# Projected keys and queries through DRAM scratch: heads outermost against one row per head and feature

## The chip, the cores and the metric

One Trainium2 chip, one of its cores. The metric is the device time of one execution in microseconds (us), as the median of several runs; lower is better. The engines are TensorE (PE, its weight loads PEld), VectorE (DVE), ScalarE (ACT), GpSimd (POOL) and SyncE (SP), which here only issues DMAs. Sixteen DMA engines move the data.

## The reference

One layer of a decoder over 512 tokens of width 1024, in float32: a SwiGLU half-step, then a mixer, then a second SwiGLU half-step, a gated per-layer embedding and a last norm. The change lies in the mixer, whose projections are:

```python
z = rmsnorm(h, norm_mix[i]) @ w_in[i]
q, kc, vc, ksl, vsl, kw, vw, g, u = jnp.split(z, split_at, axis=-1)
q = rope(q.reshape(B, L, N_HEADS, HEAD_DIM), pos)       # 8 heads x 64
kc, ksl, kw = rope(...)                                  # 2 heads x 64 each
o_nsa = nsa_attention(q, kc, vc, ksl, vsl, kw, vw, gates, pe_k, pe_v, wk1, wk2, wv1, wv2)
o_s5 = s5_mixer(u, ...)
h = h + concatenate([o_nsa, o_s5]) @ w_out[i]
```

`rope` turns features r and r + 32 of a head (a pair) against each other. Attention has three branches with the same queries: over compressed blocks of keys (`kc`, through a small two-layer network `compress`), over selected blocks (`ksl`) and over a window (`kw`). Scores are dot products over the 64 features of a head, so any order of the features gives the same scores as long as queries and keys share it. `compress` multiplies keys by rows of `wk1`, so its rows, the position table and the columns of `wk2` have to follow the order too.

## The kernel before, in words

Activations lie with features on partitions and the 512 tokens along the row. Every float32 product is three TensorE passes over operands split into a high and a low part: ACT casts the high part of a weight tile (`hi`, L147), DVE subtracts to get the low part (`lo`, L149), and PE runs `hi*xh`, `hi*xl`, `lo*xh` (`mm3`). Weight tiles come in from `wpack` in the order of use, through a ring of four buffers, issued from ACT's queue.

The mixer (L688 on) begins with the projections. `proj` makes one 128 x 512 product of 24 matmuls. `rotary` (L845) makes two of them, `oa` with the first halves of four heads (partition 32 h + r) and `ob` with the second halves, and forms `a1 = oa cos - ob sin` in buffer `r1` and `a2 = oa sin + ob cos` in `r2` on DVE (L854 to L859). The next products need both halves of one head on the 64 partitions of a contraction, and twice, on partitions 0 to 63 and 64 to 127. That move goes through DRAM: SP stores `a1` and `a2` into a scratch tensor (L860, L861), `kd` for keys and `qd` for queries, and later loads 64 rows at a time back, each twice: `kf` for keys (L868, L869; from these ACT casts `KA`, L870, and DVE makes `KB`, L871) and `qf` for the queries of one block of 128 tokens (L1031, L1032 in `scores`; from these `QA` and `QB`, L1033 to L1035). `cmp_kv` (L875) does the same for the compressed keys (`kcd`, L885) and stores the compressed values to `vcd` (L891); `windows` (L918) loads both back (`cst`, L922, L923).

Before the change the scratch is laid out by feature, then head, then token: `kd[64, 4, 512]`, `qd[64, 8, 512]`, `kcd[64, 2, 512]`. A store of 128 partitions therefore has two strides on the DRAM side, heads outermost:

```python
nc.sync.dma_start(dst[0:32].rearrange("r h t -> h r t"), a1)    # L860, 4 x 32 x 512
nc.sync.dma_start(kcd[32 * half:32 * half + 32].rearrange("r g t -> g r t"), ...)   # L885, 2 x 32 x 512
```

The order of work: keys (`kq`, one `rotary` and four `kf` tiles), queries of heads 0 to 3, the four products of the S5 input (`s5_input`, which stores `ut` to `ud`, L760, and reads it back as `u8` in 16 small loads, L764), queries of heads 4 to 7, then the S5 recurrence woven with `scores(3)`, `scores(2)`, `cmp_kv` and `v_gates`. A scheduler orders the instructions of each engine when the program is built; each engine then runs its list in order, and an instruction that waits holds all behind it on its engine. Buffers `r1` and `r2` are single and are used by every `rotary`, by `qf` of `scores(3)` and by `cst`; `ra` and `ut` have two buffers each.

Of the kernel before, what the change touches and what calls it, by code (L numbers as in the profile page):

```python
# [76 lines left out]
def block_kernel(ctx: ExitStack, tc: tile.TileContext, a: dict, out: bass.AP):  # L77
# [602 lines left out]
    nm = state["n"]  # L680

    ud = dram.tile([512, 8, 64], F32, tag="ud", name="ud")
    qd = dram.tile([64, 8, SEQ], F32, tag="qd", name="qd")
    kd = dram.tile([64, 4, SEQ], F32, tag="kd", name="kd")
    kcd = dram.tile([64, 2, SEQ], F32, tag="kcd", name="kcd")
    vcd = dram.tile([2, 64, SEQ], F32, tag="vcd", name="vcd")

    def mixer(ctx):  # L688
# [156 lines left out]
        def rotary(dst, tag):  # L845
            oa = proj(tag)
            if not hasattr(nm, "rb"):
                nm.finish()
                for t, raw in zip((cosr, sinr), ropes):
                    V.tensor_tensor(t, raw, nm.rb, OP.mult)  # L850
            yield
            ob = proj(tag)
            a1, b1, a2, b2 = (tp.tile([128, SEQ], F32, tag=n, name=n) for n in ("r1", "rb1", "r2", "r3"))
            V.tensor_tensor(a1, oa, cosr, OP.mult)  # L854
            V.tensor_tensor(a2, oa, sinr, OP.mult)
            V.tensor_tensor(b1, ob, sinr, OP.mult)
            V.tensor_tensor(b2, ob, cosr, OP.mult)
            V.tensor_tensor(a1, a1, b1, OP.subtract)
            V.tensor_tensor(a2, a2, b2, OP.add)  # L859
            nc.sync.dma_start(dst[0:32].rearrange("r h t -> h r t"), a1)  # L860
            nc.sync.dma_start(dst[32:64].rearrange("r h t -> h r t"), a2)  # L861
            yield

        def kq():
            yield from rotary(kd, "A")
            for b in range(4):
                kf = mp.tile([128, SEQ], F32, tag="ra", name="kf", bufs=2)
                nc.sync.dma_start(kf[0:64], kd[:, b])  # L868
                nc.sync.dma_start(kf[64:128], kd[:, b])  # L869
                S.copy(KA[:, b], kf)  # L870
                V.tensor_tensor(KB[0:64, b], kf[0:64], KA[0:64, b].bitcast(F32), OP.subtract)  # L871
            yield from rotary(qd[:, 0:4], "B")


        def cmp_kv():  # L875
            o = proj()
            ta = mp.tile([128, SEQ], F32, tag="ra", name="ra", bufs=2)
            tb = tp.tile([128, SEQ], F32, tag="rb1", name="rb1")
            V.tensor_tensor(ta, o, cosr, OP.mult)
            V.tensor_tensor(tb[0:64], o[64:128], sinr[64:128], OP.mult)  # L880
            V.tensor_tensor(tb[64:128], o[0:64], sinr[0:64], OP.mult)
            V.tensor_tensor(ta[0:64], ta[0:64], tb[0:64], OP.subtract)
            V.tensor_tensor(ta[64:128], ta[64:128], tb[64:128], OP.add)
            for half in range(2):
                nc.sync.dma_start(kcd[32 * half:32 * half + 32].rearrange("r g t -> g r t"),  # L885
                                  ta[64 * half:64 * half + 64])
            yield
            o = proj()
            ta = mp.tile([128, SEQ], F32, tag="ra", name="ra", bufs=2)
            V.tensor_tensor(ta, o, nm.rb, OP.mult)  # L890
            nc.sync.dma_start(vcd.rearrange("g d t -> (g d) t"), ta)  # L891
            yield
# [25 lines left out]
        def windows(src, i, dst):  # L918
            ev = []
            for g in range(2):  # L920
                st = tp.tile([128, SEQ], F32, tag=f"r{g + 1}", name="cst")
                nc.sync.dma_start(st[0:64], src[:, g])  # L922
                nc.sync.dma_start(st[64:128, 0:SEQ - 1], src[:, g, 1:SEQ])  # L923
                ev.append(st.rearrange("p (j l r) -> p l j r", l=8, r=2)[:, :, :, 0])
            sp = []
            for half, t in enumerate(dst):
                t = t.rearrange("p (l g j) -> p l g j", l=8, g=2)
                for g in range(2):
                    V.tensor_tensor(t[:, :, g], ev[g],
                                    pe[:, i, 8 * half:8 * half + 8, None].to_broadcast([128, 8, 32]), OP.add)  # L930
                sp.append(t)
            return sp

        def cmp_all():

            kt = [tp.tile([128, SEQ], F32, tag=n, name="cs") for n in ("rb1", "r3")]
            sps = windows(kcd, 0, kt), windows(vcd.rearrange("g d t -> d g t"), 1, (cosr, sinr))
            ps = bank("A", (128, 256))
            for l in range(16):
                if l % 2 == 0:  # L940
                    raw = unit(True)
                lo, n = l // 8, 64 - l // 8
                for i in range(2):
                    xs = sps[i][lo][:, l % 8].rearrange("p g j -> p (g j)")[:, lo:64]
                    w = (2 * i + l % 2) * 256
                    mm(ps[64 * i:64 * i + n], xs, raw[:, w:w + 256], l == 0, l == 15)
                if l % 2:
                    yield
            ht = tp.tile([128, SEQ], F32, tag="r3", name="ht")[:, :256]
            gelu2(ht, ps, 256, "rb1")  # L950
            pt = bank("C", (128, 2, 128))
            for m in range(2):
                PE.transpose(pt[:, m], ht[:, m * 128:m * 128 + 128], ident)
            hid = npool.tile([128, SEQ], F32, tag="acc", name="chid", bufs=1)[:, :256].rearrange("p (m c) -> p m c", m=2)
            S.activation(hid, pt, AF.Copy, scale=0.5)
            hk, hv = hid[:, :, 0:63], hid[:, :, 64:127]
            p = bank("D", (64, 2, 32))
            for m in range(2):
                mm(p.rearrange("p g j -> p (g j)")[:, 0:63], w2[:, 0, m], hk[:, m], m == 0, m == 1)
            p = p[:, :, 0:31]  # L960
            kah = KAc[:, 0:128].rearrange("p (g i j) -> p g i j", g=2, i=2)
            kbl = KBc[:, 0:64].rearrange("p (g j) -> p g j", g=2)
            S.copy(kah[0:64, :, 0, 0:31], p)
            S.copy(kah[64:128, :, 0, 0:31], p)
            V.tensor_tensor(kbl[0:64, :, 0:31], p, kah[0:64, :, 0, 0:31].bitcast(F32), OP.subtract)
            V.tensor_copy(kah[0:64, :, 1, 0:31], kbl[0:64, :, 0:31].bitcast(F32))
            for g in range(2):
                p = bank("D", (31, 64))
                for m in range(2):
                    mm(p, hv[:, m, 32 * g:32 * g + 31], w2[:, 1, m], m == 0, m == 1)  # L970
                S.copy(VLc[0:31, g, 0:64], p)
                V.tensor_tensor(VLc[0:31, g, 64:128], p, VLc[0:31, g, 0:64].bitcast(F32), OP.subtract)
# [47 lines left out]
        def scores(qb, env, pool, tags="B", stage=("ra", "ra")):  # L1020
# [2 lines left out]
            tq = slice(qb * 128, (qb + 1) * 128)  # L1023
            QA = pool.tile([128, 8, 128], FR, tag="QA", name="QA", bufs=2)
            QB = pool.tile([128, 8, 128], FR, tag="QB", name="QB", bufs=2)
            for hs, st in zip((slice(0, 4), slice(4, 8)), stage):
                if st == "ra":
                    qf = mp.tile([128, 4, 128], F32, tag=st, name="qf", bufs=2)
                else:
                    qf = tp.tile([128, 4, 128], F32, tag=st, name="qf")  # L1030
                nc.sync.dma_start(qf[0:64], qd[:, hs, tq])  # L1031
                nc.sync.dma_start(qf[64:128], qd[:, hs, tq])  # L1032
                S.activation(QA[:, hs], qf, AF.Copy, scale=0.125)  # L1033
                V.tensor_scalar(QB[0:64, hs], qf[0:64], 0.125, None, OP.mult)
                V.scalar_tensor_tensor(QA[64:128, hs], qf[64:128], 0.125, QA[64:128, hs].bitcast(F32),  # L1035
                                       OP.mult, OP.subtract)
# [139 lines left out]
        def drain(g):  # L1176
            for _ in g:
                pass
# [5 lines left out]
        s5g, pg, cg, gg = s5_all(), chain(cmp_kv(), v_gates()), cmp_all(), glu()  # L1184
        sg = chain(scores(3, envs[3], mp, TS, G3), scores(2, envs[2], mp, TS, G2))
        drain(s5_input())
        drain(rotary(qd[:, 4:8], "B"))
        table.append(tc.keep_in_program_order(S.preload_act_table_set("exp_and_others")))
        weave((s5g, 17), (sg, S1), (pg, 6))
        drain(s5g)  # L1190
# [161 lines left out]
def _pack_weights(x):  # L1352
# [49 lines left out]
    add(vt[:, 3:6])  # L1402
    add(vt[:, 6:8])
    wk, wv = (x[n][0].reshape(16, 128, 256).transpose(1, 0, 2) for n in ("cmp_wk1", "cmp_wv1"))
    for i in range(8):
        add(np.concatenate([wk[:, 2 * i:2 * i + 2], wv[:, 2 * i:2 * i + 2]], axis=1))
    m_major(x["s5_w_glu"][0], range(4), range(4))
# [4 lines left out]
    m_major(x["w_ple_gate"][0], range(8), range(8))  # L1412
    assert [len(t) // 128 for t in units] == UNIT_W
    return np.concatenate(units)


def _rope_tables():
# [6 lines left out]
def prep(x):  # L1424
# [21 lines left out]
    def pair(r, i):  # L1446
# [2 lines left out]
    sg = np.ones((128, 2), f32)  # L1449
    sg[:64, 0] = -1  # L1450
    sg[64:, 1] = -1
    pe = np.stack([x["cmp_pe_k"][0].reshape(16, 128).T, x["cmp_pe_v"][0].reshape(16, 128).T], axis=1)
    w2 = np.stack([x["cmp_wk2"][0].reshape(2, 128, 64).transpose(1, 0, 2),
                   x["cmp_wv2"][0].reshape(2, 128, 64).transpose(1, 0, 2)], axis=1)
    return {
        "xT": c(x["x"][0].T),
# [37 lines left out]
```

## Time and profile before

| | |
|---|---|
| median of 3 runs | 1091.61 us (1091.03 to 1093.57) |
| the profiled execution | 1090.99 us, of which the span from first to last instruction is 1089.1 us |
| mean granted TensorE clock | 0.985 |
| PE busy | 1042.0 us, 96% |
| DVE busy | 775.2 us, 71% |
| ACT busy | 462.1 us, 42% |
| the stretch of the mixer's projections and scores | about 400 to 545 us |

Busy time of PE counts a matmul at whatever clock it had, so a stretch at half clock is busy too. Of a timeline the start of each instruction says most: where two matmuls of the same kind start 0.227 us apart, the clock is the upper level; where they start 0.43 us apart, it is the lower. The share of the DMA engines is a mean over sixteen, so one engine busy all the time is 0.06.

### The profile page before, as it was taken

The page shows a single profiled execution, that of the slowest core. Times are in us where ns is not written, and L with a number is a line of the kernel's source. Part 1 is how long each engine was busy: PE and PEld are TensorE (multiplying, and loading weights), DVE is VectorE, ACT ScalarE, POOL GpSimd, SP SyncE. Part 2 cuts the span into 40 slices and gives each one's busy share as a digit, 9 for nine tenths or more (in the row PEclk, how much of TensorE's full clock was granted, in tenths as well). Part 3 has the DMA queues.
Part 4 walks back from the last instruction along what each step waited for, and adds up shares of the span by engine and source line. Part 5 has one row for each costly group of instructions (what it writes and reads, how often), then busy time and mean ns, then how long its engine had stood idle before and what let it go on. Part 6 is the DMA issues. An engine that isn't in the chain of part 4 may idle for free.

```text
span 1089.1 us, 15119 instructions
## 1 busy us (share of the span) xinstructions
PE 1042.0 (96%) x5854; PEld 881.4 (81%) x5854; DVE 775.2 (71%) x1328; ACT 462.1 (42%) x786; POOL 163.9 (15%) x187
## 2 busy tenths in 40 slices
PE   7999999999999998899799999999999999999995
PEld 6888888888888886676577668799899899899895
DVE  6995455445447764689788977997598678687766
ACT  6222233123222522236657875555256245245541
POOL 4006056435628200000000000000000000000000
PEclk9999999999999999999799999999999999999998
DMA  7333225336734835758121004333333423424402
GB/s 251 120 102 109 89 93 171 97 97 168 170 95 129 280 104 158 189 174 294 39 69 48 1 20 145 93 113 115 97 101 102 128 78 100 133 79 149 137 6 78
DMA packets 48596, 128.48 MB, mean 118 GB/s; under 512 B 10300, under 2 KB 17052, under 8 KB 47500
## 3 DMA queue, kind: packets, MB, share of 16 engines
q10 hardware_dynamic: 26080, 90.51, 26.5%
q0 software_dynamic: 4336, 17.60, 6.1%
q1 hardware_dynamic: 18108, 19.40, 5.7%
q8 instruction: 46, 0.75, 0.3%
q14 instruction: 26, 0.21, 0.1%
HBM read 111.99 MB, written 15.73 MB: 117 GB/s over the span
## 4 chain that ended last, share of the span: by engine, by line
PE 78%; DVE 8%; DMA 5%; issue 4%; ACT 4%; SPq 0%; POOLq 0%; POOL 0%; ACTq 0%; DVEq 0%
PE ps_C L126 24%; PE ps_A L126 23%; PE ps_B L126 21%; PE ps_D L126 10%; DMA kf<-kd 1%; DVE nmax L1053 1%; DMA kd<-r 1%; DVE lo L149 1%; DMA qd<-r 1%; ACT e L743 1%; DMA qf<-qd 1%; ACT eh L743 1%; ACT ps_B L743 1%; DMA cst<-vcd 1%; DVE el L1148 0%
## 5 line engine op out<-in xcount | busy, mean ns | idle before, releaser
L147 ACT CAST hi<-raw 128x1024 fp32r<-128x1024 f32 (+2 forms) x148 | 153.8, 1041 | 341.7 <-PE ps_C L126 125.2
L149 DVE TENSOR_TENSOR lo<-raw,hi 128x1024 fp32r<-128x1024 f32 (+2 forms) x148 | 191.2, 1294 | 55.8 <-ACT hi L147 55.1
L126 PE MATMUL ps_C<-hq,hi 128*128 128x512 f32 x704 | 217.2, 390 | 0.7 <-DVE h L404 0.7
L126 PEld LDWEIGHTS ps_C<-hq,hi 128*128 128x128 f32 x704 | 131.5, 188 | 28.2 <-DVE h L404 1.5
L126 PE MATMUL ps_A<-xh,hi 128*128 128x512 f32 (+1 forms) x376 | 132.9, 353 | 7.1 <-ACT xh L170 6.1
L126 PE MATMUL ps_C<-hq,lo 128*128 128x512 f32 x352 | 137.0, 389 | 0.0
L126 PE MATMUL ps_A<-xh,lo 128*128 128x512 f32 (+1 forms) x376 | 132.0, 351 | 1.7 <-DVE lo L149 1.7
L126 PE MATMUL ps_A<-xl,hi 128*128 128x512 f32 (+1 forms) x376 | 132.7, 353 | 1.0 <-DVE xl L222 0.8
L126 PE MATMUL ps_B<-xh,lo 128*128 128x512 f32 (+1 forms) x280 | 103.6, 370 | 4.3 <-DVE lo L149 4.3
L126 PE MATMUL ps_B<-xh,hi 128*128 128x512 f32 (+1 forms) x280 | 103.2, 369 | 0.9 <-ACT hi L147 0.9
L126 PE MATMUL ps_B<-xl,hi 128*128 128x512 f32 (+1 forms) x280 | 102.8, 367 | 0.0
L264 POOL TENSOR_TENSOR ri<-ms,negh 128x4 f32<-128x4 f32 (+1 forms) x6 | 5.5, 921 | 583.2 <-DVE ms L263 583.2
L126 PEld LDWEIGHTS ps_A<-xh,hi 128*128 128x128 f32 x376 | 71.6, 190 | 17.4 <-ACT xh L170 6.1
L404 DVE SCALAR_TENSOR_TENSOR h<-ps_C,h 128x512 f32<-128x512 f32 x64 | 43.9, 689 | 55.6 <-PE ps_C L126 55.4
L126 PEld LDWEIGHTS ps_A<-xl,hi 128*128 128x128 f32 x376 | 71.5, 190 | 12.6 <-DVE xl L222 2.4
L126 PEld LDWEIGHTS ps_A<-xh,lo 128*128 128x128 f32 x376 | 71.6, 190 | 11.0 <-DVE lo L149 1.9
L147 ACT CAST hi<-s 128x1024 fp32r<-128x1024 f32 x40 | 42.1, 1053 | 86.8 <-PE ps_D L126 40.5
L126 PEld LDWEIGHTS ps_C<-hq,lo 128*128 128x128 f32 x352 | 66.1, 188 | 13.7
L126 PEld LDWEIGHTS ps_B<-xh,lo 128*128 128x128 f32 x280 | 53.1, 190 | 13.7 <-DVE lo L149 5.1
L126 PEld LDWEIGHTS ps_B<-xh,hi 128*128 128x128 f32 x280 | 53.1, 190 | 10.1 <-ACT hi L147 1.3
L149 DVE TENSOR_TENSOR lo<-s,hi 128x1024 fp32r<-128x1024 f32 x40 | 49.0, 1225 | 16.5 <-ACT hi L147 15.8
L126 PEld LDWEIGHTS ps_B<-xl,hi 128*128 128x128 f32 x280 | 53.0, 189 | 8.8 <-issue 0.2
(402 smaller groups left out, 2314.4 us busy)
## 6 DMA issues: line engine op xcount, KB each, us to landing
raw<-in_wpack ACTq DMA_DIRECT2D x168, 512.0 KB, 3.7
sc<-s5d POOLq DMA_DIRECT2D x8, 1024.0 KB, 7.4
raw<-in_wpack SPq DMA_DIRECT2D x4, 512.0 KB, 8.3
h<-in_xT SPq DMA_DIRECT2D x8, 256.0 KB, 4.6
s5d<-fs POOLq DMA_DIRECT2D x1, 2048.0 KB, 11.7
s5d<-gt POOLq DMA_DIRECT2D x1, 2048.0 KB, 12.7
s5d<-tcs POOLq DMA_DIRECT2D x2, 1024.0 KB, 8.6
qf<-qd SPq DMA_DIRECT2D x16, 128.0 KB, 5.1
```

The lines of the kernel that those rows point to most:

```text
L126: return PE.matmul(o, lhsT, rhs, start=start, stop=stop, **kw)
L147: S.copy(hi[:, c], raw[:, c])
L149: V.tensor_tensor(lo[:, c], raw[:, c], hi[:, c].bitcast(F32), OP.subtract)
L264: G.tensor_tensor(ri, ms, negh[:, :nb], OP.pow)
L404: V.scalar_tensor_tensor(h[:, m, :], o, 0.5, h[:, m, :], OP.mult, OP.add)
L743: S.activation(*args, **kw)
L1053: V.tensor_reduce(mc, s_, AX.X, OP.max, negate=True)
```

## The change

The scratch is laid out by head, pair and half, then token: `kd[128, 2, 512]`, `qd[2, 128, 2, 512]` (its first index is the group of four heads) and `kcd[64, 2, 512]` with (head, pair) as rows. Row 32 h + r, half a, is where partition 32 h + r of `a1` or `a2` goes, so a store has one stride over 128 rows. A head's 64 features come back in the order (pair, half), so they are interleaved instead of first halves, then second halves. The rows of `cmp_wk1`, the position table of keys and the columns of `cmp_wk2` are put in the same order on the host. Values keep their order, and the loads bring the same number of bytes in the same number of rows.

```diff
-    qd = dram.tile([64, 8, SEQ], F32, tag="qd", name="qd")
-    kd = dram.tile([64, 4, SEQ], F32, tag="kd", name="kd")
+    qd = dram.tile([2, 128, 2, SEQ], F32, tag="qd", name="qd")
+    kd = dram.tile([128, 2, SEQ], F32, tag="kd", name="kd")
...
-            nc.sync.dma_start(dst[0:32].rearrange("r h t -> h r t"), a1)
-            nc.sync.dma_start(dst[32:64].rearrange("r h t -> h r t"), a2)
+            nc.sync.dma_start(dst[:, 0], a1)
+            nc.sync.dma_start(dst[:, 1], a2)
...
-                nc.sync.dma_start(kf[0:64], kd[:, b])
-                nc.sync.dma_start(kf[64:128], kd[:, b])
+                src = kd[32 * b:32 * b + 32].rearrange("r a t -> (r a) t")
+                nc.sync.dma_start(kf[0:64], src)
+                nc.sync.dma_start(kf[64:128], src)
...
-                nc.sync.dma_start(kcd[32 * half:32 * half + 32].rearrange("r g t -> g r t"),
-                                  ta[64 * half:64 * half + 64])
+                nc.sync.dma_start(kcd[:, half], ta[64 * half:64 * half + 64])
...
+                src = qd[i].rearrange("(h r) a t -> (r a) h t", h=4)[:, :, tq]
...
-                nc.sync.dma_start(qf[0:64], qd[:, hs, tq])
-                nc.sync.dma_start(qf[64:128], qd[:, hs, tq])
+                nc.sync.dma_start(qf[0:64], src)
+                nc.sync.dma_start(qf[64:128], src)
...
+    wk = _pairs(wk.reshape(2, 64, 16, 256), 1).reshape(128, 16, 256)
...
+def _pairs(v, axis):
+
+    return np.take(v, np.arange(64).reshape(2, 32).T.reshape(-1), axis=axis)
```

The lists of PE, ACT and POOL are the same in both kernels, row for row. On SP and DVE the built order differs at one place each.

SP's queue from the second pair of query stores on, before (the number behind a name tells buffers apart: `qf_3484` and `qf_3490` are heads 0 to 3 and 4 to 7 of the last block of tokens, `qf_3887` heads 0 to 3 of the block before):

```order
L860 DMA qd_2979<-r1_3443 4x32x512
L861 DMA qd_2979<-r2_3445 4x32x512
L1031 DMA qf_3887<-qd_2979 64x4x128
L1031 DMA qf_3484<-qd_2979 64x4x128
L1032 DMA qf_3484<-qd_2979 64x4x128
L1031 DMA qf_3490<-qd_2979 64x4x128
L1032 DMA qf_3490<-qd_2979 64x4x128
L1032 DMA qf_3887<-qd_2979 64x4x128
L885 DMA kcd_2981<-ra_3528 2x32x512 x2
```

and in the changed kernel:

```order
L861 DMA qd_2979<-r1_3443 128x512
L862 DMA qd_2979<-r2_3445 128x512
L1033 DMA qf_3887<-qd_2979 64x4x128
L1034 DMA qf_3887<-qd_2979 64x4x128
L1033 DMA qf_3484<-qd_2979 64x4x128
L1034 DMA qf_3484<-qd_2979 64x4x128
L1033 DMA qf_3490<-qd_2979 64x4x128
L1034 DMA qf_3490<-qd_2979 64x4x128
L887 DMA kcd_2981<-ra_3528 64x512 x2
```

The second load of `qf_3887` has moved up four places, ahead of the four loads of the last block; the shapes of the stores are the other difference.

DVE's list in the same part of the program, the end of the compressed keys' rotation (`ra`) and the low parts of the queries, before:

```order
L789 TENSOR_TENSOR t_3551<-ps_C,sc 64x256
L1034 TENSOR_SCALAR QB<-qf 64x512 x2
L882 TENSOR_TENSOR ra<-ra,rb_3529 64x512
L883 TENSOR_TENSOR ra<-ra,rb_3529 64x512
L1034 TENSOR_SCALAR QB<-qf 64x512
```

and in the changed kernel:

```order
L790 TENSOR_TENSOR t_3551<-ps_C,sc 64x256
L884 TENSOR_TENSOR ra<-ra,rb_3529 64x512
L1036 TENSOR_SCALAR QB<-qf 64x512 x2
L885 TENSOR_TENSOR ra<-ra,rb_3529 64x512
L1036 TENSOR_SCALAR QB<-qf 64x512
```

One subtraction of the compressed keys now stands ahead of two `QB` instructions that it stood behind.

## Rows read from the trace of the kernel before

**Rows 1.** The page's first part: busy time and share of each engine.

```profile
PE 1042.0 (96%) x5854; PEld 881.4 (81%) x5854; DVE 775.2 (71%) x1328; ACT 462.1 (42%) x786; POOL 163.9 (15%) x187
```

**Rows 2.** Timeline of PE, two places: start, length, instruction [idle before, releaser].

```profile
427.86 0.39 PE L126 MATMUL ps_B<-xl,hi 128*128 128x512 f32 x1
432.52 0.79 PE L126 MATMUL ps_B<-xh,lo 128*128 128x512 f32 x1 [4.27 <-DVE lo L149]
433.11 0.63 PE L126 MATMUL ps_B<-xh,hi 128*128 128x512 f32 x1
433.54 0.63 PE L126 MATMUL ps_B<-xl,hi 128*128 128x512 f32 x1
...
439.19 1.00 PE L126 MATMUL ps_C<-u,sc 128*128 128x64 f32 x8
...
456.24 0.29 PE L126 MATMUL ps_A<-hi,xl 128*128 128x280 f32 x1
456.37 0.29 PE L126 MATMUL ps_A<-hi,xh 128*128 128x280 f32 x1
461.52 0.79 PE L126 MATMUL ps_B<-KA,QA 128*128 128x512 f32 x1 [4.86 <-DVE QA L1035]
...
466.61 0.29 PE L126 MATMUL ps_A<-hi,xh 128*128 128x280 f32 x1
```

**Rows 3.** Timeline of DVE, the same columns, 411 to 533 us.

```profile
411.80 0.69 DVE L854 TENSOR_TENSOR r<-ps_B,cosr 128x512 f32<-128x512 f32 x1 [3.64 <-DMA kd<-r]
416.18 0.69 DVE L855 TENSOR_TENSOR r<-ps_B,sinr 128x512 f32<-128x512 f32 x1 [3.69 <-DMA kd<-r]
...
430.39 1.02 DVE L758 TENSOR_TENSOR ut<-ps_A,rb 128x512 f32<-128x512 f32 x1 [7.71 <-DMA ud<-ut]
...
439.75 0.68 DVE L856 TENSOR_TENSOR rb<-ps_B,sinr 128x512 f32<-128x512 f32 x1
...
470.39 0.42 DVE L1034 TENSOR_SCALAR QB<-qf 64x512 fp32r<-64x512 f32 x1 [0.84 <-DMA qf<-qd]
471.83 0.69 DVE L1035 SCALAR_TENSOR_TENSOR QA<-qf,QA 64x512 fp32r<-64x512 f32 x1 [0.69 <-ACT QA L1033]
...
532.70 0.42 DVE L1034 TENSOR_SCALAR QB<-qf 64x512 fp32r<-64x512 f32 x1 [2.07 <-DMA qf<-qd]
```

**Rows 4.** Timeline of SP's queue: start and length of the issues, not of the transfers.

```profile
404.50 0.69 SPq L860 DMA_DIRECT2D kd<-r  x1
405.30 0.53 SPq L861 DMA_DIRECT2D kd<-r  x1
...
446.37 0.55 SPq L861 DMA_DIRECT2D qd<-r  x1
446.97 6.28 SPq L1031 DMA_DIRECT2D qf<-qd  x2
```

**Rows 5.** Stretches: length, busy us of PE, PEld, DVE, ACT, POOL, clock, DMA share, GB/s.

```profile
439.75:465.76 26.01, 21.15 (x116) 17.18 (x116) 18.81 (x41) 5.90 (x9) 0.72 (x2) 0.88 0.64 180
450.00:453.00 3.00, 3.00 (x18) 2.50 (x16) 2.92 (x6) 0.00 (x0) 0.00 (x0) 1.00 0.26 102
470.00:530.00 60.00, 52.37 (x385) 36.42 (x384) 54.04 (x129) 34.60 (x82) 2.69 (x9) 0.97 0.60 200
```

**Rows 6.** DMA issues by tensor: count, KB each, median us to landing.

```profile
qf<-qd SPq DMA_DIRECT2D x16, 128.0 KB, 5.1
pled<-et SPq DMA_DIRECT2D x8, 256.0 KB, 2.7
```

**Rows 7.** Line 760's four stores of `ud`, 256 KB each, 128 rows.

```profile
DMA to landing us min/median/max: 3.6/6.8/10.1
```

**Rows 8.** Waits of DVE, 439.75 to 466 us: total, times, longest.

```profile
DVE QB L1034 <- DMA qf<-qd: 4.6, 2, 2.4
...
DVE QA L1035 <- ACT QA L1033: 0.4, 1, 0.4
```

**Rows 9.** Longest wait of SP's queue behind a store of compressed keys.

```profile
SPq L1031 <- DMA kcd<-ra: 8.6, 1, 8.6
```

More of the change, by code (lines that the diff above doesn't have):

```diff
@@ L867, in kq @@
                 kf = mp.tile([128, SEQ], F32, tag="ra", name="kf", bufs=2)
-                nc.sync.dma_start(kf[0:64], kd[:, b])
-                nc.sync.dma_start(kf[64:128], kd[:, b])
+                src = kd[32 * b:32 * b + 32].rearrange("r a t -> (r a) t")
+                nc.sync.dma_start(kf[0:64], src)
+                nc.sync.dma_start(kf[64:128], src)
                 S.copy(KA[:, b], kf)
                 V.tensor_tensor(KB[0:64, b], kf[0:64], KA[0:64, b].bitcast(F32), OP.subtract)
-            yield from rotary(qd[:, 0:4], "B")
+            yield from rotary(qd[0], "B")
         def cmp_kv():
@@ L921, in windows @@
                 st = tp.tile([128, SEQ], F32, tag=f"r{g + 1}", name="cst")
-                nc.sync.dma_start(st[0:64], src[:, g])
-                nc.sync.dma_start(st[64:128, 0:SEQ - 1], src[:, g, 1:SEQ])
+                nc.sync.dma_start(st[0:64], src[g])
+                nc.sync.dma_start(st[64:128, 0:SEQ - 1], src[g, :, 1:SEQ])
                 ev.append(st.rearrange("p (j l r) -> p l j r", l=8, r=2)[:, :, :, 0])
@@ L936, in cmp_all @@
             kt = [tp.tile([128, SEQ], F32, tag=n, name="cs") for n in ("rb1", "r3")]
-            sps = windows(kcd, 0, kt), windows(vcd.rearrange("g d t -> d g t"), 1, (cosr, sinr))
+            sps = windows(kcd.rearrange("(g r) a t -> g (r a) t", g=2), 0, kt), windows(vcd, 1, (cosr, sinr))
             ps = bank("A", (128, 256))
@@ L1025, in scores @@
             QB = pool.tile([128, 8, 128], FR, tag="QB", name="QB", bufs=2)
-            for hs, st in zip((slice(0, 4), slice(4, 8)), stage):
+            for i, (hs, st) in enumerate(zip((slice(0, 4), slice(4, 8)), stage)):
+                src = qd[i].rearrange("(h r) a t -> (r a) h t", h=4)[:, :, tq]
                 if st == "ra":
@@ L1186, in mixer @@
         drain(s5_input())
-        drain(rotary(qd[:, 4:8], "B"))
+        drain(rotary(qd[1], "B"))
         table.append(tc.keep_in_program_order(S.preload_act_table_set("exp_and_others")))
@@ L1451, in prep @@
     sg[64:, 1] = -1
-    pe = np.stack([x["cmp_pe_k"][0].reshape(16, 128).T, x["cmp_pe_v"][0].reshape(16, 128).T], axis=1)
-    w2 = np.stack([x["cmp_wk2"][0].reshape(2, 128, 64).transpose(1, 0, 2),
+    pe = np.stack([_pairs(x["cmp_pe_k"][0], 1).reshape(16, 128).T, x["cmp_pe_v"][0].reshape(16, 128).T], axis=1)
+    w2 = np.stack([_pairs(x["cmp_wk2"][0], 1).reshape(2, 128, 64).transpose(1, 0, 2),
                    x["cmp_wv2"][0].reshape(2, 128, 64).transpose(1, 0, 2)], axis=1)
```

## The prediction

> **What bounds the kernel now.** I read the page first, then PE's timeline for gaps, and then followed each gap back through the engine that released it. PE is busy 96% of the span [rows 1], so whatever this change gives has to come out of the few places where PE stands still, and one must see which of those hang on the scratch stores. Two do [rows 2].
>
> The first is at 427.86 us: PE has begun the second product of the last four query heads and waits 4.27 us for a low part `lo`. DVE makes that `lo` right behind `ut` (L758), and in front of `ut` it stood idle for 7.71 us, because the buffer of `ut` was still being stored to `ud` [rows 3]. One step further back DVE had already stood 3.64 and 3.69 us, once for each half of the key store `kd`, since `r1` and `r2` are single buffers. The two `kd` stores were issued at 404.50 and 405.30 [rows 4] and let go of DVE at 411.80 and 416.18, so they took 7.3 and 10.9 us.
>
> The second is at 456.37: PE waits 4.86 us for the queries `QA`. Their loads had to wait until the second pair of `qd` stores had left `r1` and `r2`. The last of these was issued at 446.37, and SP then sat over the next two issues, one of which waits for a store, for 6.28 us [rows 4].
>
> After each stop PE runs at the lower clock for a while: matmuls of 512 columns start 0.43 us apart (433.11 to 433.54) where they otherwise start 0.227 apart, which is what 1.2 against 2.4 GHz makes [rows 2].
>
> Why are the stores slow? From 450 to 453 us the second `qd` store is the only transfer in hand: the DMA engines are busy to 0.26 and move 102 GB/s [rows 5]. A share of 0.26 of sixteen is four engines, and the store's DRAM side is 4 x 32 x 512, with four heads outermost. At 102 GB/s, 256 KB take 2.6 us of pure transfer, and whatever is queued behind on those four engines waits. Stores of 128 x 512 with the same bytes show a median of 2.7 us to landing [rows 6]. So my reading is that the store is spread over as many DMA engines as its outermost size allows.
>
> **The change part by part.** The stores keep their number (two `kd`, four `qd`, two `kcd`), bytes and rows of 2 KB; what changes is that 128 (or 64) rows stand outermost. How long such a store takes at this place no row shows. From below it is 2.7 us [rows 6]; from above 10.1 us, the slowest `ud` store, which has the new shape but was queued behind the slow `qd` stores [rows 7]. I take 3.6, the fastest `ud` store, which comes from the same stretch with weight traffic beside it.
>
> *Keys.* The `kd` stores land at 404.50 + 3.6 = 408.1 and 408.9 instead of 411.8 and 416.2. DVE's work up to `ut` and the low part comes some 7 us sooner. The `ud` stores no longer have slow stores in front of them, so `lo` is ready near 419 us, against 427.86 + 0.23 when PE asks for it. Even at 6.8 us for each store it is ready near 426. The first stop goes. From 427.86 to 439.19 PE starts 23 matmuls, which at 0.227 take 5.2 us of the 11.3: **6.1 us**, idle time and lost clock together.
>
> *Queries.* The product now ends at 433.1, so DVE's part of the rotation (439.75 before [rows 3]) begins near 433.4. It issues the two `qd` stores near 436.3 and 438, they land near 440 and 441.6, and the loads `qf` follow at 5.1 us [rows 6], near 446. PE asks for `QA` at 456.37 - 6.1 = 450.3. Before, 10.24 us pass from 456.37 to 466.61. They hold two score groups (two matmuls of 0.23 us and a mask of 0.07) and 13 matmuls 0.13 us apart, with small changes between kinds some 2.9 us: up to **7.3 us** for PE. But DVE has to come along. From there to its first maximum of scores, at 465.76, it has 18.8 us of work in 26.0 [rows 5], and only 4.6 + 0.4 = 5.0 us of the idle time hang on `qf` [rows 8]; the rest waits for weights cast by ACT behind PE. DVE therefore allows 5.0, not 7.3, and from here to 530 us it is the tighter engine (54.0 of 60 us busy, PE 52.4 [rows 5]). I take **5.0**.
>
> *Compressed keys.* SP stands 8.6 us behind the `kcd` store [rows 9], with the next queries and the compressed keys queued behind it. This delays `QB` by 0.84 and `QA` by 0.69 us [rows 3]: **1.5 us**, as DVE is the bound there.
>
> *Order.* Moving the second half of `qf_3887` up puts one issue of about 0.6 us in front of the loads PE waits for, and the moved subtraction one DVE instruction of 0.7 us. Both lie inside the 3 to 4 us by which `QA` is early. I cost them at nothing. Without that cover they cost 1.3 us.
>
> *Loads.* Bytes and row sizes stay; heads now lie 128 KB apart instead of 2 KB, features 2 KB instead of 16 KB. I take no change. The Trainium skill speaks against long strides: "DMA: Bandwidth & Descriptors", section "Latency and other measured facts", has copies with row pitches of large powers of two fall from 214 to 103 GB/s at pitches of 4 MiB, though its smallest pitch, 512 KiB, still gives 207; no row here has such a pitch, and I leave the sum alone for it.
>
> Sum: 6.1 + 5.0 + 1.5 = 12.6 us. Against the profiled execution, 1090.99 us (span 1089.1 and 1.9 around it), this is 1078.4. The median of the runs is 0.6 above that execution, so I forecast **1079.0 us**. The bounds of the store move this little: at 2.7 us DVE still sets the pace; at 6.8 us the queries are about 3 us late and 2 to 4 us come back. If PE's 7.3 holds, 2.3 more are won. Its own range is 1076 to 1083.
>
> **The rivals.**
>
> *Only the first stop goes.* The queries' path is long (two stores, SP's queue, loads, ACT, DVE), and DVE could reach `QA` late for its own work. 18.8 us of work from 433.4 on, with some 2 us of waits for weights, speaks for it; the 3 to 4 us that I found to spare speak against. Gain 6.1: 1085.5 us.
>
> *The waits behind also go.* The later `qf` loads (2.07 us at 532.70 [rows 3]) and the full 7.3 us of PE come on top: 12.6 + 2.1 + 2.3 = 17, 1074.6 us. Against it: those later loads wait for a buffer, not for a store.
>
> *The change does not do what it says.* If the DRAM writes and not the count of engines hold the store at 102 GB/s, everything stays: 1091.6 us. Against it stand the `pled` stores.
>
> *The loads become slower, and the kernel with them.* The four pieces of 512 bytes per partition now lie 128 KB apart. If a `qf` load takes X us longer, DVE pays at three places: X less 3 to spare at 455.88, X less 1.8 at 470.39 and all of X at 532.70. This eats 12.6 us when 3X = 17.4, at X = 5.8, a landing of 10.9 instead of 5.1 us. At X = 7 the loss is 16.2 and the time 1095 us. For it: small pieces, much idle time of DMA in them. Against it: within a head the rows are now contiguous, where they were 16 KB apart.
>
> *The loads halve their rate.* As a mechanism of this kernel, 5.1 us becomes 10.2: X = 5.1, a loss of 10.5, 1089.5 us. This is what the pitch rule of the Trainium skill would make of it, were 128 KB already a large pitch.
>
> **How the numbers follow.** Forecast 0.60, only the first stop 0.15, more than forecast 0.12, no effect 0.06, halved rate 0.04, slower 0.03. The range 1074 to 1086 holds the first three with the bounds of the store, and leaves out less than 2 in 10. A difference of 0.2% is 2.2 us, about what a measurement can tell from none. Faster by more: 0.60 + 0.15 + 0.12 = 0.87, and half of the halved rate, 0.89. Same: 0.06 and the other half, 0.08. Slower: 0.03.
>
> **What would show it.** In the profile after, each `kd`, `qd` and `kcd` store should land in 3 to 5 us; DVE should have no wait over 1 us behind `kd` or `ud`; PE should run through the eight products of the projections without the stops at 427.86 and 456.37, at full clock. From 470 us on everything should stand about 12 us earlier, in the same order, and the last 400 us should be as before. I am wrong if the stores land sooner and PE still stops for `QA`, if the `qf` loads take over 8 us, or if the gain made by 470 us has been given back by 645.

## The result, and the profile after

The changed kernel takes **1077.67 us** (median of 4 runs, 1077.02 to 1083.12), the kernel before 1091.32 beside it (4 runs, 1090.09 to 1093.57): a ratio of 0.9884, 95% interval 0.9848 to 0.992. The profiled execution took 1077.02 us, its span is 1075.2 us against 1089.1, so 13.9 us are to be found. The mean granted clock is 0.988.

The page's first part after answers to [rows 1]: PE has lost 3.5 us of busy time, and the other 10.4 us were standstill. The 3.5 fit the clock: a mean of 0.985 over 1089.1 us leaves 16.3 us missing at full clock, 0.988 over 1075.2 leaves 12.9, which is 3.4 less.

```profile
PE 1038.5 (97%) x5854; PEld 879.3 (82%) x5854; DVE 775.6 (72%) x1328; ACT 462.3 (43%) x786; POOL 162.8 (15%) x187
```

PE's timeline after, at the matmuls of [rows 2] (start, length, instruction, [idle before, releaser]):

```profile
427.67 0.39 PE L126 MATMUL ps_B<-xl,hi 128*128 128x512 f32 x1
427.90 0.39 PE L126 MATMUL ps_B<-xh,lo 128*128 128x512 f32 x1
...
432.89 1.00 PE L126 MATMUL ps_C<-u,sc 128*128 128x64 f32 x8
...
450.07 0.29 PE L126 MATMUL ps_A<-hi,xh 128*128 128x280 f32 x1
450.20 0.39 PE L126 MATMUL ps_B<-KA,QA 128*128 128x512 f32 x1
...
452.94 0.29 PE L126 MATMUL ps_A<-hi,xh 128*128 128x280 f32 x1
...
470.52 0.44 PE L126 MATMUL ps_D<-sc,xx 128*64 128x128 f32 x4 [2.12 <-DVE xx L802]
```

Both stops are gone and the clock stays up: `xh,lo` follows 0.23 us behind, where 4.27 us of waiting stood, and `KA,QA` 0.13 us behind, where 4.86 stood. Taking each matmul's start from its start in [rows 2] gives the account. At 427.67 the change is 0.19 us ahead, at 432.89 it is 6.30, so the first stop gave **6.1**. At 450.07 it is still 6.30 ahead, at 452.94 it is 13.67: the second stop gave **7.4**. The wait for `xx` at 470.52 stands in the kernel before too, and there the change is 14.0 ahead; at the end it is 13.9. PE's timeline before, at that wait:

```profile
484.53 0.44 PE L126 MATMUL ps_D<-sc,xx 128*64 128x128 f32 x4 [1.74 <-DVE xx L801]
```

DVE's timeline after, at the places of [rows 3]:

```profile
408.43 0.69 DVE L855 TENSOR_TENSOR r<-ps_B,cosr 128x512 f32<-128x512 f32 x1 [0.46 <-DMA kd<-r]
...
416.76 1.10 DVE L759 TENSOR_TENSOR ut<-ps_A,rb 128x512 f32<-128x512 f32 x1 [0.83 <-PE ps_A L126]
...
433.08 0.69 DVE L857 TENSOR_TENSOR rb<-ps_B,sinr 128x512 f32<-128x512 f32 x1 [3.02 <-PE ps_B L126]
...
445.77 0.75 DVE L1036 TENSOR_SCALAR QB<-qf 64x512 fp32r<-64x512 f32 x2
...
447.72 1.29 DVE L1037 SCALAR_TENSOR_TENSOR QA<-qf,QA 64x512 fp32r<-64x512 f32 x2
...
452.23 1.26 DVE L1055 TENSOR_REDUCE nmax<-ps_B 128x1 f32<-128x512 f32 x2
...
456.05 0.42 DVE L1036 TENSOR_SCALAR QB<-qf 64x512 fp32r<-64x512 f32 x1
...
456.83 0.69 DVE L1037 SCALAR_TENSOR_TENSOR QA<-qf,QA 64x512 fp32r<-64x512 f32 x1
...
468.26 0.58 DVE L930 TENSOR_TENSOR cosr<-cst,pe 128x256 f32<-128x256 f32 x1 [2.72 <-DMA cst<-vcd]
...
518.81 0.42 DVE L1036 TENSOR_SCALAR QB<-qf 64x512 fp32r<-64x512 f32 x1 [2.15 <-DMA qf<-qd]
```

The two waits of 3.64 and 3.69 us for `kd` are one of 0.46. In front of `ut`, where DVE waited 7.71 us for a store, it waits 0.83 for PE. The waits in front of `QB` and `QA` are gone up to 470 us; the one at 532.70 [rows 3] is still there, at 518.81 with 2.15 us. Two waits behind a DMA have grown. That for the compressed values went from 1.72 us (at 482.26 before) to 2.72. And DVE now waits 3.34 us at 422.26 for `KA`, which ACT casts from the `kf` loads; before, it came to this place so late (432.39) that it did not wait. The `lo` that PE needs at 427.90 was made before that (417.71, 1.21 us long), so this one costs PE nothing.

The same stretch of DVE as the first of [rows 5], from the rotation to the first maximum of scores, after (columns as there):

```profile
433.08:452.23 19.15, 19.15 (x118) 15.89 (x117) 18.64 (x40) 5.70 (x9) 0.72 (x2) 1.00 0.77 219
```

It took 26.01 us with 18.81 of work. Now it takes 19.15 with 18.64: DVE has no time left to give in it.

The DMA issues after (KB each, median us to landing):

```profile
qf<-qd SPq DMA_DIRECT2D x16, 128.0 KB, 3.1
...
kf<-kd SPq DMA_DIRECT2D x8, 128.0 KB, 4.9
qd<-r SPq DMA_DIRECT2D x4, 256.0 KB, 3.3
ud<-ut SPq DMA_DIRECT2D x4, 256.0 KB, 3.8
...
kd<-r SPq DMA_DIRECT2D x2, 256.0 KB, 4.1
...
kcd<-ra SPq DMA_DIRECT2D x2, 128.0 KB, 2.7
```

The stores land in 2.7 to 4.1 us where 3.6 was taken; `ud`, whose stores are unchanged, fell from 6.8 [rows 7], and the loads `qf` from 5.1 [rows 6]. The loads `kf` went the other way, from a median of 3.1 to 4.9; why is not shown, but e7 below, with the old layout, has 4.1, so it is not the new layout alone.

### The profile page after: what moved, and what is told of

Its sections match the earlier page's. It is cut to its first block, busy times and chain, and to the rows that moved or that the text cites. A ratio compares the mean times of both kernels' runs of the same rounds, so it can differ in the third digit from the quotient of the medians.

```text
span 1075.2 us, 15120 instructions
## 1 busy us (share of the span) xinstructions
PE 1038.5 (97%) x5854; PEld 879.3 (82%) x5854; DVE 775.6 (72%) x1328; ACT 462.3 (43%) x786; POOL 162.8 (15%) x187
## 2 busy tenths in 40 slices
DMA packets 48696, 128.48 MB, mean 119 GB/s; under 512 B 10400, under 2 KB 17152, under 8 KB 47600
## 4 chain that ended last, share of the span: by engine, by line
PE 82%; DVE 8%; issue 4%; ACT 4%; DMA 2%; POOLq 0%; POOL 0%; DVEq 0%; SPq 0%; ACTq 0%
PE ps_C L126 24%; PE ps_A L126 24%; PE ps_B L126 22%; PE ps_D L126 11%; DVE nmax L1055 1%; DVE lo L149 1%; ACT e L744 1%; DMA raw<-in_wpack 1%; DMA cst<-vcd 1%; ACT eh L744 1%; ACT ps_B L744 1%; DVE el L1150 0%; ACT oh L998 0%; DVE QA L1037 0%; DVE vv L794 0%
## 5 line engine op out<-in xcount | busy, mean ns | idle before, releaser
L126 PEld LDWEIGHTS ps_A<-xl,hi 128*128 128x128 f32 x376 | 71.4, 190 | 12.6 <-DVE xl L222 2.4
```

The costliest lines, as they stand in the source:

```text
L126: return PE.matmul(o, lhsT, rhs, start=start, stop=stop, **kw)
```

## Experiments

Each ratio is to the kernel before, run beside it on the same chip. Two such series were run, with 1093.07 us (13 runs) and 1094.72 us (7 runs) as the medians of the kernel before. The intervals are about 0.3% to either side, 3 to 4 us, so small differences between experiments are read from the traces and not from the ratios. A trace is one execution of four (ten for e1), though, and its time within them is given where the argument hangs on it. The times in the expectations were set against 1091 us for the kernel before; in the two series it took about 2 and 3 us more.

### Is it the spread or the layout?

**e1** keeps the new layout and makes its stores narrow again: behind each head's 32 rows lies a row that nothing uses, so the store's DRAM side is 4 x 32 x 512 (`kcd` 2 x 32 x 512). The order of its instructions is that of the kernel before on every engine.

```diff
-    kd = dram.tile([128, 2, SEQ], F32, tag="kd", name="kd")
+    kd = dram.tile([4, 33, 2, SEQ], F32, tag="kd", name="kd")
...
-            nc.sync.dma_start(dst[:, 0], a1)
+            nc.sync.dma_start(dst[:, :, 0] if len(dst.shape) == 4 else dst[:, 0], a1)
```

> The new layout, with one unused row of scratch behind each head, so that every store is 4 x 32 x 512 (compressed keys 2 x 32 x 512) again while rows, row sizes and loads stay those of the change. Theory (a store runs on as many DMA engines as its outermost size): all of the gain goes, about 1091 us, the kd stores land after 7 and 11 us, PE stops again for a low part (about 4 us) and for QA (about 5 us). Rival (the layout itself is what is faster, heads and features closer together in DRAM): 1078 us, stores landing in 3 to 4 us.

Measured: 1092.55 us (10 runs), ratio 0.9996 (0.9982 to 1.001): the whole gain is gone. Both stops of PE are back, in PE's timeline of e1:

```profile
432.07 0.79 PE L126 MATMUL ps_B<-xh,lo 128*128 128x512 f32 x1 [3.40 <-DVE lo L149]
...
460.86 0.80 PE L126 MATMUL ps_B<-KA,QA 128*128 128x512 f32 x1 [4.73 <-DVE QA L1037]
```

and so is the stretch in which the second `qd` store (issued at 446.43) is alone:

```profile
449.50:452.50 3.00, 3.00 (x18) 2.50 (x18) 2.92 (x6) 0.00 (x0) 0.00 (x0) 1.00 0.26 94
```

The DMA engines are again busy to 0.26, four of sixteen, with rows that lie as in the change but for the unused ones. With its order of instructions that of before, e1 differs from the kernel before in the layout alone, and the layout gave nothing: the number of rows outermost decides, and not where they lie. The Trainium skill states this as a rule ("DMA: Bandwidth & Descriptors", section "Why a DMA increments its semaphore by 16 and not by 1"): the transfer runs on the largest number of engines up to 16 that divides the slowest dimension of both sides. That gives 4 for 4 x 32 x 512 and 16 for 128 x 512; this trace agrees with 0.26 for the first.

**e7** is the converse: the layout of before and its order of instructions on every engine, but with partition 4 r + h, so that 32 features stand outermost in the store of four heads (`kd` has a fifth head per feature that nothing uses, and its store goes out as 32 x 4 x 512). **e2** is e7 with the `kcd` store left at 2 x 32 x 512.

```diff
-            nc.sync.dma_start(dst[0:32].rearrange("r h t -> h r t"), a1)
+            nc.sync.dma_start(dst[0:32], a1)
...
-                nc.sync.dma_start(kcd[32 * half:32 * half + 32].rearrange("r g t -> g r t"),
+                nc.sync.dma_start(kcd[32 * half:32 * half + 32],
```

> The kernel before with its old scratch layout and its own order of instructions on every engine, SP's too, but with partition 4 r + h in the projections of keys and queries and 2 r + g in that of the compressed keys, so that key and query stores are 32 x 4 x 512 and the compressed keys are 64 x 512. The compressed keys are rotated by other pairs' angles, which is the part that is computed otherwise. Theory (only the outermost size of the stores counts; neither layout nor the two moved places on SP and DVE do): as the change, 1077 to 1079 us. Rival (part of the gain is the new layout's contiguous heads or the moved instructions): 1082 us or more.

Measured: 1081.19 us (1077.99 to 1085.19), ratio 0.9883 (0.9847 to 0.992), the ratio of the change to 0.0001. Its span is 1076.2 us, and PE has no wait for `lo` or `QA`. In us the median lies between what the theory and the rival named; the ratio and the trace are on the theory's side. So the layout in DRAM and the moved rows on SP and DVE are worth nothing that can be measured here (the two spans differ by 1.0 us, and the intervals of the ratios reach 4 us to either side); the spread of the stores is the gain.

The page's count of DMA packets tells the same without a time: 48596 before and in e1, 48696 in the change and in e7. The kernels below with one kind of store narrow lie between: 24 packets below the change with two stores at four outermost (e3, e8), 48 below with four (e4), 28 below with the two `kcd` stores at two outermost (e5, and e2). So each store has 12 packets fewer at 4 and 14 fewer at 2 outermost than with 32 or more, all of them under 512 bytes. That is 16 - 4 and 16 - 2: it fits one small packet for each engine that takes part, and sixteen engines for 32 rows as for 128.

> The kernel before with its layout by feature, head, token, and only the columns of the projection put in another order: partition 4 r + h instead of 32 h + r, so that a key or query store is 32 x 4 x 512 with two strides in DRAM. The compressed keys keep their narrow store, and are rotated by the angles of other pairs here, which is the part that is computed otherwise. Theory (outermost size counts): most of the gain is there, 1078 to 1080 us, because 32 rows outermost take all sixteen engines. Rival (one stride over 128 rows is what is needed, two strides are slow): 1091 us. Rival (the layout matters): 1091 us.

Measured: 1085.58 us, ratio 0.9921 (0.9895 to 0.9948): neither the theory's time nor the rivals', as none of them priced the `kcd` store that stayed narrow. The stops in the projections are gone, but the next queries now come late behind that store, in DVE's timeline of e2:

```profile
463.25 0.42 DVE L1034 TENSOR_SCALAR QB<-qf 64x512 fp32r<-64x512 f32 x1 [6.27 <-DMA qf<-qd]
```

0.84 us before [rows 3] has become 6.27: what was hidden behind the other two stops came out when they went. PE, too, now waits 2.98 us at 460.04 for `sc`, a load of 1 MB from POOL's queue; e5 below has the same.

### One kind of store narrow at a time

The next four are the change with one kind of store narrow, by the edit of e1 (the order of SP's queue is the change's in all four; DVE's order is that of before in e4 and e8): **e3** the keys (`kd`), **e4** the queries (four `qd` stores), **e5** the compressed keys (`kcd`), **e8** the second pair of `qd` alone.

```diff
-    kd = dram.tile([128, 2, SEQ], F32, tag="kd", name="kd")           # e3
+    kd = dram.tile([4, 33, 2, SEQ], F32, tag="kd", name="kd")
...
-    qd = dram.tile([2, 128, 2, SEQ], F32, tag="qd", name="qd")        # e4, e8
+    qd = dram.tile([2, 4, 33, 2, SEQ], F32, tag="qd", name="qd")
...
-    kcd = dram.tile([64, 2, SEQ], F32, tag="kcd", name="kcd")         # e5
+    kcd = dram.tile([2, 33, 2, SEQ], F32, tag="kcd", name="kcd")
```

> The change with only the two kd stores at 4 x 32 x 512. The prediction's chain (late kd stores hold DVE, and with it the low part that PE waits for at the first stop): 1083.8 us, the first stop is back whole (6.1 us). Rival (ud is late because it is queued behind the slow stores of the first queries; kd alone leaves the low part at about 427, just in time): 1078 to 1079 us and no stop of PE over 1 us in the projections.

Measured: 1082.23 us, ratio 0.9905 (0.9876 to 0.9934). DVE's timeline of e3 has the waits for `kd` back, but the one in front of `ut` is small:

```profile
411.05 0.69 DVE L855 TENSOR_TENSOR r<-ps_B,cosr 128x512 f32<-128x512 f32 x1 [3.16 <-DMA kd<-r]
416.18 0.69 DVE L856 TENSOR_TENSOR r<-ps_B,sinr 128x512 f32<-128x512 f32 x1 [4.44 <-DMA kd<-r]
423.19 1.09 DVE L759 TENSOR_TENSOR ut<-ps_A,rb 128x512 f32<-128x512 f32 x1 [0.91 <-DMA ud<-ut]
```

PE does not stop for `lo`: with slow `kd` stores alone DVE is in time. What came was a part of the second stop (1.92 us for `QA` at 452.70). So the prediction's chain fails here, but the rival's "no stop of PE over 1 us" does too, and its 1078 to 1079 us.

> The change with only the four qd stores at 4 x 32 x 512. Theory: the second stop (PE waits for QA) is back, 7.2 us of PE time, and the first is not, since kd lands at 409 and leaves 8 us more for ut and the low part: about 1085 us. Rival (the first stop hangs on the stores of the first queries in front of ud): both stops, 1090 to 1091 us.

Measured: 1085.38 us, ratio 0.9928 (0.99 to 0.9956). Now `ut` waits, in DVE's timeline of e4:

```profile
423.69 1.09 DVE L759 TENSOR_TENSOR ut<-ps_A,rb 128x512 f32<-128x512 f32 x1 [7.66 <-DMA ud<-ut]
```

It is almost the full wait of 7.71 us, yet it ends 6.7 us earlier than the 430.39 of [rows 3], since DVE was not late before it; `lo` is in time and the first stop stays away. **So the first stop needs both**: late keys and `ud` stores behind slow `qd` stores. (No run has just `kd` and `qd` narrow. In e1 `kcd` is narrow as well, but its stores are issued only at 456.69.) The second comes back in pieces, 2.06 us for `QA` and 1.57 and 0.87 for what is late next, in PE's timeline of e4:

```profile
452.82 0.50 PE L126 MATMUL ps_B<-KA,QA 128*128 128x512 f32 x1 [2.06 <-DVE QA L1037]
...
456.81 0.60 PE L126 MATMUL ps_A<-hi,xh 128*128 128x280 f32 x1 [1.57 <-ACT hi L147]
...
458.28 0.60 PE L126 MATMUL ps_A<-hi,xh 128*128 128x280 f32 x1 [0.87 <-DVE ra L891]
```

> The change with only the second pair of query stores at 4 x 32 x 512. Theory (the second stop hangs on this pair alone): PE waits 2 to 5 us for QA and then runs slowly for some us, 1083 to 1085 us, as with all four query stores narrow. Rival (in that kernel it was the first pair, in front of ud, that made DVE and ACT late): 1078 to 1080 us.

Measured: 1081.13 us (1078.88 to 1085.15), ratio 0.9893 (0.9856 to 0.993); span 1077.0 us, 1.8 above the change. DVE waits 1.75 us for `qf` at 447.32 and PE does not stop for `QA`. The second pair alone does not make the second stop either. In e4 DVE was late already when it formed the queries that this pair stores: the first half (L859) starts at 437.72, in e8 at 435.67, because DVE waited 1.99 us at 436.77 for a cast of ACT. The time lies between what the theory and the rival named.

> The change with only the two stores of the compressed keys at 2 x 32 x 512. The prediction's term (they cost DVE 0.84 + 0.69 us): 1079.2 us, 1.5 above the change. Rival (with everything else early there is nothing left to hide them: the next queries, queued behind them on SP, come some 6 us late, as in the kernel with features outermost, where DVE waited 6.27 us for them): 1083 to 1086 us, DVE waits over 4 us for a qf load near 460 us.

Measured: 1082.59 us, ratio 0.99 (0.9869 to 0.9931). DVE's timeline of e5:

```profile
460.65 0.42 DVE L1036 TENSOR_SCALAR QB<-qf 64x512 fp32r<-64x512 f32 x1 [4.15 <-DMA qf<-qd]
```

The wait near 460 us is the rival's, and its 1083 to 1086 us are just missed. The stores that I priced at 1.5 us cost about 5 by then in this execution: the wait for `xx` that ends at 470.52 in the change ends at 475.70 in e5. It is not SP's queue alone that they hold up. In this stretch of e5 no other queue moves anything, and the DMA engines are busy to 0.13, two of sixteen, at half the rate of a store with four outermost:

```profile
449.00:450.00 1.00, 1.00 (x8) 1.00 (x9) 0.94 (x3) 0.00 (x0) 0.27 (x1) 1.00 0.13 47
```

The 1 MB load `sc`, issued from POOL at 448.65, lands after 9.9 us, where it takes 5.5 in the change (issued at 448.17), and PE itself waits for it, in PE's timeline of e5:

```profile
458.60 0.66 PE L126 MATMUL ps_C<-u,sc 128*128 128x64 f32 x4 [2.04 <-DMA sc<-s5d]
```

So a narrow store delays a wide transfer of another queue as well. How much of the 5 us each way is worth is not shown.

**The parts do not add up.** How far a kernel is behind the change, at the matmul behind that wait for `xx` and at the end of the span. All of it is from one profiled execution each: for the change the fastest of its four, for e3 and e5 the slowest of their four, for e1 the third of its ten.

| narrow stores | start of that matmul, us | behind the change there | behind it at the end |
|---|---|---|---|
| all (e1) | 484.30 | 13.8 | 13.5 |
| `kd` (e3) | 474.73 | 4.2 | 9.6 |
| `qd` (e4) | 477.88 | 7.4 | 8.6 |
| `kcd` (e5) | 475.70 | 5.2 | 9.0 |
| second pair of `qd` (e8) | 472.31 | 1.8 | 1.8 |

Up to there the three parts make 16.8 in these executions against 13.8 for all. Behind it e3, e4 and e5 lose another 5.4, 1.2 and 3.8 us, and e1 loses nothing. The medians do not bear out that the parts cost more than the whole: by the ratios e3, e4 and e5 lie 0.0021, 0.0044 and 0.0016 above the change, about 2, 5 and 2 us, together 9, and e1 lies 0.0112 above, 12 us. With intervals of 3 to 4 us either sum could be the larger; that the parts have no fixed prices rests on the waits above, not on these sums.

Where the profiled execution of e3 loses its time behind the wait goes with the clock; stretches of e3 (columns as in [rows 5]):

```profile
470.00:475.00 5.00, 2.92 (x25) 2.82 (x25) 2.91 (x7) 1.34 (x3) 0.00 (x0) 0.97 0.22 51
475.00:480.00 5.00, 5.00 (x24) 2.77 (x21) 4.90 (x13) 2.43 (x7) 0.64 (x2) 0.50 0.08 16
480.00:485.00 5.00, 5.00 (x24) 2.90 (x24) 4.83 (x12) 1.49 (x5) 0.00 (x0) 0.50 0.72 244
```

and of the change:

```profile
470.00:475.00 5.00, 4.48 (x36) 2.89 (x38) 4.94 (x15) 2.85 (x8) 0.65 (x2) 1.00 0.15 23
475.00:480.00 5.00, 4.58 (x41) 2.69 (x37) 4.87 (x12) 2.73 (x7) 0.00 (x0) 1.00 0.86 309
```

For ten us behind the wait PE has the lower clock in e3 (24 matmuls in 5 us against 41). The same two stretches from 475 us on have 0.54 and 0.50 in e5, and 0.83 and 0.50 in e4. Of the 5.4 us of e3 the last 1.5 come at a second dip, 0.50 from 638.6 to 642 us. That a run of e3 always has these dips is not shown: the profiled one, 1086.58 us, is the slowest of its four, and the fastest took 1079.55.

### The wait that is left

**e6** tries to beat the change: the loads of the compressed values (`cst`) stand on SP ahead of the last four `qf` loads, against the wait of 2.72 us that had grown.

```diff
+                with tc.issue_after(last_cst[0].ins) if last_cst else nullcontext():
                     nc.sync.dma_start(qf[0:64], src)
                     nc.sync.dma_start(qf[64:128], src)
```

> The change, with the four qf loads of the last two blocks, which nothing reads for 50 us, moved on SP behind the four loads of the compressed values; no other engine's order changes. Theory (the 2.7 us that DVE waits for those values is queueing behind the 512-byte pieces of the four qf loads, and DVE is the bound there): 1075 to 1076 us and no wait of DVE over 1 us for cst. Rival (the values are held by the loads of the S5 tables from POOL's queue, or PE and ACT are the bound by then): 1077.7 us.

Measured: 1077.97 us (1076.56 to 1079.66), ratio 0.9853 (0.9824 to 0.9881), an interval that overlaps the change's; span 1074.8 us. DVE waits as before, in its timeline of e6:

```profile
468.01 0.59 DVE L932 TENSOR_TENSOR cosr<-cst,pe 128x256 f32<-128x256 f32 x1 [2.38 <-DMA cst<-vcd]
```

SP had issued these loads at 460.26 to 463.08, no earlier than the change (460.16 to 462.99), although they now stand first: so it is not the `qf` loads that hold them. They land in up to 7.4 us. A load of 1 MB, `sc`, goes out from POOL at 459.63, right in front of them, and lands after 7.8 us, at 467.4; DVE's wait for the values ends at 468.01. In the change it is 459.52, 7.9 us and 468.26. This fits the rival; that `sc` is what slows them was not tried. No version that beats the change was found.

## Why the prediction was right

The forecast was 1079.0 us, in the range of 1074 to 1086 and for the right reason, but two of the three terms were off, by +2.4 and -1.2 us, and in part cancelled: that the sum came as near as it did is partly luck.

- **The spread of a store.** Right: e1 and e7 show it from both sides, and the stretch at 0.13 and the packet counts put numbers to two, four and sixteen engines. The landing of 3.6 us stands among 2.7 to 4.1.
- **Keys, 6.1.** Measured 6.1, with the clock as foreseen, and `lo` was ready at 418.92 where the text said near 419. The path was told too simply: it made the slow `kd` stores the start of the chain and `ud` a consequence. e3 and e4 show two causes that only together make the stop.
- **Queries, 5.0.** Measured 7.4. The failed step is "DVE therefore allows 5.0, not 7.3", with its reason "the rest waits for weights cast by ACT behind PE". In the trace of before ACT's timeline shows what those casts waited for, and DVE's what came of the second:

```profile
437.52 1.05 ACT L147 CAST hi<-raw 128x1024 fp32r<-128x1024 f32 x1 [3.60 <-DMA u<-ud]
441.85 0.90 ACT L147 CAST hi<-raw 128x840 fp32r<-128x840 f32 x1 [3.27 <-DMA u<-ud]
...
442.78 1.03 DVE L149 TENSOR_TENSOR lo<-raw,hi 128x840 fp32r<-128x840 f32 x1 [1.75 <-ACT hi L147]
```

  and after the change

```profile
427.42 1.06 ACT L147 CAST hi<-raw 128x1024 fp32r<-128x1024 f32 x1 [2.58 <-PE ps_B L126]
432.86 0.89 ACT L147 CAST hi<-raw 128x840 fp32r<-128x840 f32 x1 [4.38 <-PE ps_B L126]
```

  Before, ACT was held by loads of `ud` (in front of each cast it issues a weight tile, at 437.09 and 441.44, and the wait ended there). SP had issued these loads from 430.99 and 439.10 on, 12 and 10 us later than in the change (419.05 and 429.09), behind the late `ud` stores, and DVE's `lo` at 442.78 waited 1.75 us for the second cast. With the spread they wait for PE alone, and this wait of DVE went as well: 5.0 + 1.75 is 6.75 of the 6.86 us by which the stretch shortened (26.01 to 19.15). DVE also began it 6.67 us earlier (439.75 to 433.08), not 6.1. So PE's own limit of 7.3 was the one that held, a case that the prediction had named and priced ("If PE's 7.3 holds").
- **Compressed keys, 1.5.** From 452.94 to 470.52 PE won 0.3 us net. The waits of 0.84 and 0.69 us did go, but DVE's next wait, for the compressed values, grew by 1.0. The step that failed is that nothing was named that is late next. As a price of the `kcd` stores by themselves 1.5 looks too low: the trace of e5 makes it about 5 where the other stores are fast. The medians are less sure of it: by the ratios it is about 2 us (e5 to the change) and 4 (e2 to e7), with 3 to 4 us of noise. A wait in a trace that has larger waits in front of it shows only what those leave of it.
- **Order.** Right: costed at nothing, and e7 with the order of before has the ratio of the change. The cover was thinner than the "3 to 4 us" said: the first two `QA` end at 449.01, 1.2 us before PE asks at 450.20.
- **Loads.** Right that the `qf` loads would not slow; they became faster, 5.1 to 3.1 us, with nothing slow queued in front of them. For the pitch rule of the Trainium skill ("DMA: Bandwidth & Descriptors", section "Latency and other measured facts"), heads 128 KB apart cost nothing that shows here: e7, whose stores are as fast and whose heads lie 2 KB apart, has a median of 3.0. The `kf` loads, which the prediction did not price, slowed from 3.1 to 4.9, without a cost to PE.
- **The rivals.** *Only the first stop goes* fell with `KA,QA` at 450.20 without a wait. *The waits behind also go* was half right: PE's 7.3 came, but what it added behind did not: the wait of 2.07 us at 532.70 is still there, 2.15 at 518.81. *The change does not do what it says* fell with the landings, and both rivals on slower loads with the 3.1 us of `qf`.

The terms of the profiled execution are then 0.2 from the start of the stretch, 6.1, 7.4 and 0.3, and 0.1 lost later: 13.9, against 12.6 forecast.

## What to carry to other kernels

A DRAM access pattern with 2 or 4 outermost runs, with rows of 2 KB behind, kept a store on a few of the sixteen DMA engines here, and transfers queued behind it paid as well, in e5 even one of another queue. A DMA share near 0.25 or 0.13 while one transfer is in hand is the sign, and orders with 32, 64 or 128 rows outermost cured it. When such a cause feeds several waits, remove it everywhere: the compressed keys' stores, priced at 1.5 us beside the other slow ones, stood for about 5 us at 475 us in the trace in which they were the only ones left. And do not take a part's price from one execution: that of e3 ended 9.6 us behind the change, where its median ratio says about 2. Follow a wait "for another engine" one step further before writing it off as fixed: that engine may hang on the same slow transfer.

## What was not expected of the hardware

A wait of 2.08 us (e3, at 474.73, with PE busy 2.92 of the 5 us from 470) was followed by ten us at the lower level of the clock, 0.50. A wait of 2.12 us (the change, at 470.52) was followed by 1.00. Around that one PE was busy 4.48 of the 5 us from 470. But the busy time does not tell them apart either. In the kernel with all stores narrow (e1) the wait of 1.72 us at 484.30 came with 3.28 busy us of the 5 from 480, and 0.66 in the 5 us from 485; in the kernel before, the wait of 1.74 us at 484.53 came with 3.26, and 1.00. Nor does a dip always cost: e1 was 13.8 us behind the change before it and 13.5 at the end. So the price of a wait of PE was not its length: the profiled execution of e3 lost 5.4 us behind a wait that is as long as the one in the change. What decides is not shown.
